# Fewer and larger pieces of the small products between the projections of the recurrent heads, with landing buffers of their own for the state-space branch's matrices

## The chip, the cores and the metric

The kernel runs on one NeuronCore of a Trainium2 chip. The metric is the device time of one execution in microseconds. All data is float32. Large products are made from two fp32r halves of each operand (a high part and the remainder), so that every product of two float32 matrices is three matmuls in fp32r; the small products are plain float32 matmuls, each of which the trace shows as two matmul instructions (a transpose shows as one).

## The reference, cut to what matters

Two transformer-like blocks follow each other on 512 tokens of width 1024. The change lies in the second one, in the stage between its input projection and its gates:

```python
z = rmsnorm(h, mix_norm_g[l])
p = z @ w_in[l]                                   # 1024 -> 1024 + 4 * 1024 + 2 * 1024 columns
y_a = s5_mixer(p[..., :o1], ...)                  # the branch: a state-space recurrence
y_b = hgrn2_mixer(p[..., o1:o2], p[..., o2:o3], p[..., o3:o4], p[..., o4:o5], ...)   # q, f, i, og of 8 heads
merged = (sigmoid(p[..., o5:o6]) * (y_a @ w_ssm_proj[l])
          + sigmoid(p[..., o6:]) * (y_b @ w_hgrn_proj[l]))
```

Each of the 8 heads has width 128: f gives a decay, its running sum within chunks gives the scaled q and k, and scores, a state per chunk and an output follow. The branch takes u, the first 1024 columns, in 64 groups of 16, turns it into v (`R` times u), runs a complex recurrence over 64 steps, and multiplies back (`MO`: two 128x128 matrices per group, one for u and one for the state).

## The kernel before, in words

Everything on the core is 528 columns wide here (16 meta tokens and 512 tokens). The stage runs so:

- **u** (L1171 to L1182): four weight loads of 256 columns, 8 products, each `prod2`. `prod2` (L1116) makes one 128x528 product as two halves of 264 (or 258) columns, each with 8 k steps; a k step is the three matmuls of `mm3` (L126 to L128) and then a call of `slot` (L1104).
- **heads** (the loop at the end of the stage, `for hd in range(9)`): for each of 8 heads two weight loads of two 1024x128 matrices each (`load_w2`, L119), then `head`: the products f, og, i, q, that is 4 x 16 = 64 k steps, with the scalar and vector work of the head between them (L1275 to L1321). What is left of a head, `back` (transposes of v and of the outgoing k, scores, states, outputs, the norm, a transpose back), is a generator that is stepped while the next head's products run.
- **gates** (hd = 8): 8 weight loads, 16 products, 256 k steps, beside the last head's `back`.

`slot` steps the generators in `self.fillers`. `back` is stepped at every k step, the branch at every third one (heads 1 to 4, `s5_state`) or at every one (heads 5 to 7, `s5_out`). Each step traces a few instructions up to its next `yield`. What is not finished at the end of a head is flushed there. The generator `s5_state` has 11 pieces of matmuls on R (L1205; each 24 matmul instructions and a copy, L1206) and then 64 steps of four vector operations (L1217 to L1220). `s5_out` has 16 copies of the states by ACT (L1230), then the MO products (L1247, L1248, copy L1249), a Gelu over the whole result (L1251) and 8 stores of y (`y_d`, L1253), through POOL's queue.

The queues don't follow the traced order strictly: the layer that builds the program orders each engine's instructions itself, by the traced order and by when it reckons operands and buffers to be there, and fixes that order in the program. Each engine then runs its list in order.

Buffers: raw weights land in `wraw` (two of 1 MB); `raw()` (L86) gives every third request a place in `xraw`, one more buffer of 1 MB that exists in this stage only. R and MO ask the same `raw()`: 6 loads of 768 KB for R and 10 of up to 896 KB for MO. Weights are split by ACT (`wh`, L131) and DVE (`wl`, L132) into three buffers each. `aux` is four PSUM banks for all small products, `pp` two double banks for the projections. All these loads are issued by SP (SyncE), in the order of its list; a load waits there until its buffer is free.

Of the kernel before, what the change touches and what calls it, by code (L numbers as in the profile page):

```python
# [19 lines left out]
P = 128  # L20
# [49 lines left out]
class Kern:  # L70
# [1057 lines left out]
    def block2(self):  # L1128
# [39 lines left out]
        self.xraw, self.nraw = hp, 2  # L1168
# [20 lines left out]
        def s5_state():  # L1189
            nonlocal Hs  # L1190
            v_ = slot(2).rearrange("p a b -> p (a b)").rearrange("p (c r g) -> p c r g", c=66, r=2)
            for c0 in range(0, 32, 3):
                n = min(3, 32 - c0)
                if c0 % 6 == 0:
                    rbase = 2 * c0
                    ng = min(12, 64 - rbase)
                    Rt = self.raw().rearrange("p (g x) -> p g x", x=P)
                    nc.sync.dma_start(Rt[:, :ng], self.R_d[:, rbase : rbase + ng])
                ps = self.aux()
                p4 = ps[:, : 2 * n * 66].rearrange("p (r g c) -> p r g c", r=2, g=n)  # L1200
                for i in range(2 * n):
                    g = 2 * c0 + i
                    for r in range(2):
                        par = i % 2
                        nc.tensor.matmul(p4[64 * par : 64 * par + 64, r, i // 2], lhsT=Rt[:, g - rbase, 64 * r : 64 * r + 64], rhs=U[:, g], start=True, stop=True)  # L1205
                nc.scalar.copy(v_[:, :, :, c0 : c0 + n].rearrange("p c r g -> p r g c"), p4)  # L1206
                yield
            self.tap("v", v_)
            Hs = slot(3).rearrange("p a b -> p (a b)").rearrange("p (c r g) -> p c r g", c=66, r=2)
            e = nc.vector  # L1210
            e.tensor_copy(Hs[:, 0], v_[:, 0])
            ar = self.a8[:, 0:1, :].to_broadcast([P, 2, 32])
            ai = self.a8[:, 1:3, :]
            for c in range(1, 65):
                t1 = self.tmp.tile([P, 2, 32], F32, tag="st1", bufs=2, name=self.nm("st1"))
                t2 = self.tmp.tile([P, 2, 32], F32, tag="st2", bufs=2, name=self.nm("st2"))
                e.tensor_tensor(t1, Hs[:, c - 1], ar, ALU.mult)  # L1217
                e.tensor_tensor(t2, Hs[:, c - 1, ::-1, :], ai, ALU.mult)
                e.tensor_tensor(t1, t1, v_[:, c], ALU.add)
                e.tensor_tensor(Hs[:, c], t1, t2, ALU.add)  # L1220
                yield

        def s5_out():
            SS = slot(2).rearrange("p a b -> p (a b)").rearrange("p (g c) -> p g c", c=66)
            nc.gpsimd.memset(SS[:, :, 0:1], 0.0)
            for par in range(2):
                for r in range(2):
                    for c0 in range(0, 65, 17):
                        c1 = min(65, c0 + 17)
# [6 lines left out]
            for g0 in range(0, 64, 7):  # L1236
                n = min(7, 64 - g0)
                MO = self.raw().rearrange("p (g s x) -> p g s x", s=2, x=P)
                nc.sync.dma_start(MO[:, :n].rearrange("p g s x -> p g (s x)"), self.MO_d[:, g0 : g0 + n])
# [9 lines left out]
                nc.scalar.copy(Y[:, g0 : g0 + n], ps[:, : n * 66].rearrange("p (g c) -> p g c", g=n))  # L1249
            yield  # L1250
# [73 lines left out]
        def back(hd, I, KO, K1, KX, Q1, QI, dec, og):  # L1324
# [4 lines left out]
            def tok(src, s, out):  # L1329
                pt_ = self.aux()  # L1330
                for c in range(NT):
                    nc.tensor.transpose(pt_[:, c * P : c * P + P], ch(src)[:, c], self.ident)
                    if c % 2:
                        yield
# [6 lines left out]
                out += [o, om]  # L1341

# [7 lines left out]
            for c in range(NT):  # L1350
                for i in range(4):
# [3 lines left out]
                    if i % 2:  # L1355
                        yield
# [7 lines left out]
            yield  # L1364
# [4 lines left out]
            for c in range(3):  # L1369
                yield  # L1370
# [5 lines left out]
            for _ in range(3):  # L1376
                yield
# [22 lines left out]
            for _ in range(16):  # L1400
                yield
# [29 lines left out]
        for hd in range(9):  # L1431
            self.fillers = [[prev, 1], [s5, 3 if hd < 5 else 1]]
# [17 lines left out]
        self.xraw = None  # L1450
# [165 lines left out]
    def run(self):  # L1616
        tc, nc = self.tc, self.nc
        with ExitStack() as es:
# [8 lines left out]
            self.nraw, self.xraw = 0, None  # L1627
# [48 lines left out]
```

## Time and profile before

| | us |
|---|---|
| median of 3 runs (1820.84 to 1827.03) | 1825.83 |
| the profiled execution, its own time | 1825.45 |
| its span, first to last instruction | 1823.6 |
| PE (TensorE) busy | 1738.0 (95%) |
| DVE busy | 1074.7 (59%) |
| ACT busy | 780.4 (43%) |
| POOL busy | 321.4 (18%) |

Mean granted TensorE clock: 0.986 of full speed.

How to read it: a view of the waits names an engine's instruction, what released it, the idle time in total, how often and the longest. A view of windows gives, for a stretch, its length, the busy time of each engine with the number of instructions, then the granted clock and the DMA share. In a timeline a row begins with start and duration, and an idle time before it stands in brackets with what ended it. The duration of a matmul is that of one that is pipelined with its neighbours, so the cost of a run of matmuls is read from start to start. The chain lists what the end of the program waited for, in order of time.

### The profile page before, as it was taken

The numbers are of one execution on the slowest core, as the hardware profiler recorded it, in microseconds if no ns is written. First come the engines' busy times: TensorE is split into PE (matmuls) and PEld (weight loads), VectorE is DVE, ScalarE is ACT, GpSimd is POOL, SyncE is SP. The second block draws the span as 40 slices with busy tenths as digits, with TensorE's granted clock in tenths as the row PEclk, the third lists the DMA queues.
The fourth block names the chain that finished last, engine by engine and source line by source line (L and its number), as shares of the span: only waits on it lengthen the run. The fifth ranks groups of instructions, "written<-read, shape, count | busy, mean of one in ns | idle before, by whom it ended". The sixth has DMA issues, their size and how long they took to land.

```text
span 1823.6 us, 28508 instructions
## 1 busy us (share of the span) xinstructions
PE 1738.0 (95%) x11509; PEld 1525.5 (84%) x11509; DVE 1074.7 (59%) x2343; ACT 780.4 (43%) x1298; POOL 321.4 (18%) x441
## 2 busy tenths in 40 slices
PE   1989998999999999999999999999999999999998
PEld 1777755877777778899899899899999999889986
DVE  6687878986443566454488634343444466536652
ACT  2674485344332444324546834343322443324332
POOL 5000000278836841031000000200000000000001
PEclk9899998999999999999899999999999999999999
DMA  7323625353244325367432135936443222332231
GB/s 280 98 88 111 215 71 186 116 105 124 85 117 150 108 92 182 117 195 123 129 99 82 65 116 162 227 118 232 156 137 104 82 93 70 113 107 93 70 104 47
DMA packets 178766, 226.64 MB, mean 124 GB/s; under 512 B 10699, under 2 KB 146746, under 8 KB 175178
## 3 DMA queue, kind: packets, MB, share of 16 engines
q1 hardware_dynamic: 164256, 181.95, 31.5%
q0 software_dynamic: 10640, 38.19, 7.8%
q10 hardware_dynamic: 3738, 4.69, 0.7%
q8 instruction: 90, 1.47, 0.4%
q14 instruction: 42, 0.34, 0.1%
HBM read 196.29 MB, written 32.70 MB: 126 GB/s over the span
## 4 chain that ended last, share of the span: by engine, by line
PE 69%; issue 12%; DVE 9%; ACT 4%; DMA 4%; POOL 1%; ACTq 0%; SPq 0%; POOLq 0%; DVEq 0%
PE pp L126 18%; PE pp L127 17%; PE pp L128 17%; DVE wl L132 2%; DMA wraw<-in_w_in_dram 2%; PE pd L128 1%; PE pd L126 1%; PE pd L127 1%; PE aux L1072 1%; PE aux L1354 1%; PE aux L442 1%; PE aux L126 1%; PE aux L128 1%; PE aux L127 1%; PE pv L455 1%
## 5 line engine op out<-in xcount | busy, mean ns | idle before, releaser
L126 PE MATMUL pp<-s,wh 128*128 128x258 f32 (+2 forms) x1856 | 543.2, 293 | 8.6 <-ACT sg L1427 4.5
L127 PE MATMUL pp<-s,wh 128*128 128x258 f32 (+2 forms) x1856 | 527.9, 284 | 0.0
L128 PE MATMUL pp<-s,wl 128*128 128x258 f32 (+2 forms) x1856 | 525.5, 283 | 0.0
L132 DVE TENSOR_TENSOR wl<-wraw,wh 128x1024 fp32r<-128x1024 f32 (+4 forms) x260 | 302.9, 1178 | 190.4 <-ACT wh L131 189.4
L131 ACT CAST wh<-wraw 128x1024 fp32r<-128x1024 f32 (+4 forms) x260 | 245.0, 964 | 338.0 <-PE pp L127 203.4
L126 PEld LDWEIGHTS pp<-s,wh 128*128 128x128 f32 x1856 | 352.2, 190 | 13.3 <-ACT sg L1427 4.7
L127 PEld LDWEIGHTS pp<-s,wh 128*128 128x128 f32 x1856 | 352.9, 190 | 0.2 <-DVE s L333 0.2
L128 PEld LDWEIGHTS pp<-s,wl 128*128 128x128 f32 x1856 | 352.4, 190 | 0.1
L126 PE MATMUL pp<-h2H,wh 128*128 128x512 f32 x336 | 133.5, 397 | 2.4 <-DVE cy L846 2.4
L127 PE MATMUL pp<-h2L,wh 128*128 128x512 f32 x336 | 133.2, 396 | 1.1 <-DVE h2L L343 1.1
L128 PE MATMUL pp<-h2H,wl 128*128 128x512 f32 x336 | 132.1, 393 | 0.0
L126 PEld LDWEIGHTS pp<-h2H,wh 128*128 128x128 f32 x336 | 63.1, 188 | 20.1 <-ACT aH L131 2.8
L127 PEld LDWEIGHTS pp<-h2L,wh 128*128 128x128 f32 x336 | 63.0, 188 | 16.1 <-DVE h2L L343 2.2
L128 PEld LDWEIGHTS pp<-h2H,wl 128*128 128x128 f32 x336 | 63.2, 188 | 14.2
L126 PE MATMUL pp<-aH,wh 128*128 128x512 f32 x176 | 70.1, 398 | 0.0
L127 PE MATMUL pp<-aL,wh 128*128 128x512 f32 x176 | 69.8, 396 | 0.0
L128 PE MATMUL pp<-aH,wl 128*128 128x512 f32 x176 | 69.8, 396 | 0.0
L1592 POOL TENSOR_TENSOR ht<-ht,gf 128x512 f32<-128x512 f32 x4 | 5.7, 1438 | 344.7 <-ACT fsq L1590 344.7
L126 PE MATMUL pp<-wh,hH 128*128 128x512 f32 (+1 forms) x160 | 62.3, 389 | 1.2 <-ACT hH L525 1.2
L1556 DVE TENSOR_TENSOR xz<-pp,rb_f 128x516 f32<-128x516 f32 x44 | 30.6, 696 | 54.2 <-PE pp L128 54.2
L127 PE MATMUL pp<-wl,hH 128*128 128x512 f32 (+1 forms) x160 | 61.9, 387 | 0.5 <-DVE wl L132 0.5
L128 PE MATMUL pp<-wh,hL 128*128 128x512 f32 (+1 forms) x160 | 61.4, 384 | 0.0
(592 smaller groups left out, 3462.0 us busy)
## 6 DMA issues: line engine op xcount, KB each, us to landing
wraw<-in_w_up_dram SPq DMA_DIRECT2D x40, 1024.0 KB, 5.2
wada<-in_w_ada_dram SPq DMA_DIRECT2D x24, 1024.0 KB, 4.9
wraw<-in_w_in_dram SPq DMA_DIRECT2D x17, 1024.0 KB, 12.3
wraw<-in_w_down_dram SPq DMA_DIRECT2D x16, 704.0 KB, 4.6
wraw<-in_w_in_dram SPq DMA_DIRECT2D x22, 512.0 KB, 5.4
wraw<-in_w_down_dram SPq DMA_DIRECT2D x8, 1024.0 KB
wraw<-MO_d SPq DMA_DIRECT2D x6, 896.0 KB
xraw<-in_w_in_dram SPq DMA_DIRECT2D x10, 512.0 KB, 7.7
```

The costliest lines, as they stand in the source:

```text
L126: mm(ps, lhsT=sh, rhs=mh, start=start, stop=False)
L127: mm(ps, lhsT=sh, rhs=ml, start=False, stop=False)
L128: mm(ps, lhsT=sl, rhs=mh, start=False, stop=stop)
L131: self.nc.scalar.copy(H, x)
L132: self.nc.vector.tensor_tensor(L, x, H.bitcast(F32), ALU.subtract)
L442: nc.tensor.transpose(ps[:, w : w + P], probs[i][:, j * P : (j + 1) * P], self.ident)
L455: self.nc.tensor.matmul(pv[64 * a : 64 * a + 64, j * P :], lhsT=vs[a](j), rhs=ptrs[a][j], start=(j == 0), stop=(j == NT - 1), skip_group_c ...
L1072: nc.tensor.matmul(pk[:16, i * P : i * P + P], lhsT=W[:, gi, 0, :], rhs=Ca[:, gi, :8, :].rearrange("p l h -> p (l h)"), start=True, stop=True)
L1354: nc.tensor.matmul(p3[:n, c, 32 * i : 32 * i + 32], lhsT=lhs, rhs=ch(Q1)[:, c, 32 * i : 32 * i + 32], start=True, stop=True)
L1556: nc.vector.tensor_tensor(xz, ps, rb, ALU.mult)
L1592: nc.gpsimd.tensor_tensor(h, h, gf[:, :512], ALU.mult)
```

## The change

`raw()` loses its third buffer, so that weights land in the two `wraw` buffers only. R and MO get a tag of their own, `xr`, two buffers of 512 KB: R now comes in 11 loads of up to 384 KB and MO in 16 loads of 512 KB, each asked for one piece ahead. A generator now says with `yield n` after how many k steps it wants to go on. The pieces of `back` are joined: all four transposes of a matrix, two chunks of scores, the three states, two chunks of outputs. The MO products go by 4 groups instead of 7, in one piece. The core of the diff:

```diff
     def raw(self):
-        self.nraw += 1
-        if self.xraw is not None and self.nraw % 3 == 2:
-            return self.xraw.tile([P, WCAP], F32, tag="xraw", bufs=1, name=self.nm("xraw"))
         return self.wpool.tile([P, WCAP], F32, tag="wraw", bufs=self.wbufs[0], name=self.nm("wraw"))
...
         self.nslot += 1
         for f in list(self.fillers):
-            if self.nslot % f[1] == 0 and next(f[0], self) is self:
-                self.fillers.remove(f)
+            if self.nslot >= f[1]:
+                w = next(f[0], 0)
+                f[1] = self.nslot + w
+                if w == 0:
+                    self.fillers.remove(f)
...
+            def r_load(c0):
+                n = min(3, 32 - c0)
+                Rt = hp.tile([P, 1024], F32, tag="xr", bufs=2, ...)
+                nc.sync.dma_start(Rt, self.R_d[:, 2 * c0 : 2 * c0 + 2 * n])
+                Rts.append(Rt)
+            r_load(0)
             for c0 in range(0, 32, 3):
                 n = min(3, 32 - c0)
-                if c0 % 6 == 0:
-                    ...
-                    Rt = self.raw().rearrange("p (g x) -> p g x", x=P)
-                    nc.sync.dma_start(Rt[:, :ng], self.R_d[:, rbase : rbase + ng])
+                Rt = Rts.pop(0)
+                if c0 + 3 < 32:
+                    r_load(c0 + 3)
...
                 nc.scalar.copy(v_[:, :, :, c0 : c0 + n].rearrange("p c r g -> p r g c"), p4)
-                yield
+                yield 2
...
                 e.tensor_tensor(Hs[:, c], t1, t2, ALU.add)
-                yield
+                yield 3
...  s5_out: after each of 16 copies (L1230)
-                        for _ in range(4):
-                            yield
+                        yield 2
...
-            for g0 in range(0, 64, 7):
-                n = min(7, 64 - g0)
-                MO = self.raw().rearrange("p (g s x) -> p g s x", s=2, x=P)
-                nc.sync.dma_start(MO[:, :n]..., self.MO_d[:, g0 : g0 + n])
-                for _ in range(8):
-                    yield
+            mo_load(0)
+            for g0 in range(0, 64, 4):
+                if g0 + 4 < 64:
+                    mo_load(g0 + 4)
+                yield 7
+                MO = MOs.pop(0)
                 ps = self.aux()
-                for i in range(n):
-                    if i % 2 == 0:
-                        yield
+                for i in range(4):
                     ...
-            yield
+            yield 6
             nc.scalar.activation(Y, Y, AF.Gelu_apprx_tanh)
...  back: transposes (L1332), scores (L1354), states (L1371), outputs (L1382)
-                    if c % 2:
-                        yield
...
+                yield 4
...
-                    if i % 2:
-                        yield
+                if c == 1:
+                    yield 4
...
-                yield
                 nc.tensor.matmul(s3[:, c + 1], lhsT=KT[:, c], rhs=VT[:, c], start=True, stop=True)
...
-            for _ in range(3):
-                yield
+            yield 5
...
                 nc.tensor.matmul(o3[:, c], lhsT=ch(QI)[:, c], rhs=Sx[:, c], start=False, stop=True)
-                yield
+                if c == 1:
+                    yield 4
...
-            for _ in range(16):
-                yield
+            yield 22
...
-            self.fillers = [[prev, 1], [s5, 3 if hd < 5 else 1]]
+            self.fillers = [[prev, self.nslot + 3], [s5, self.nslot + 1]]
```

Per head, `back` had a piece at nearly each of the first 24 k steps and its last one at the 40th; now it has 7 pieces at the k steps 3, 7, 11, 15, 19, 24 and 28 and the last one at 50. The branch's state part takes 22 + 192 = 214 k steps instead of 225, its output part 32 + 112 + 6 = 150 instead of some 185 (from the start of head 5).

## Rows read from the trace of the kernel before

**Rows 1.** PE's waits from 832 to 1252 us: in total, times, longest.
```profile
PE pp L126 <- ACT sg L1427: 4.5, 1, 4.5
PE aux L1404 <- DVE KT L1397: 3.9, 4, 2.8
PE pp L126 <- ACT wh L131: 3.5, 1, 3.5
```
**Rows 2.** Windows by stage: length, PE, PEld, DVE, ACT, POOL busy, clock, DMA.
```profile
880.00:905.00 25.00, 21.05 (x325) 17.53 (x320) 15.75 (x56) 15.19 (x25) 0.00 (x0) 0.90 0.53 158
905.00:940.00 35.00, 34.69 (x260) 32.37 (x261) 27.93 (x117) 19.00 (x28) 1.13 (x2) 0.93 0.48 136
...
1008.00:1045.00 37.00, 34.17 (x264) 32.00 (x263) 22.16 (x66) 34.11 (x43) 2.39 (x5) 0.95 0.20 68
...
1176.00:1180.00 4.00, 2.32 (x11) 2.32 (x12) 2.36 (x2) 2.12 (x4) 1.08 (x2) 0.54 1.06 380
1180.00:1186.00 6.00, 6.00 (x40) 6.00 (x40) 0.09 (x1) 1.30 (x2) 0.00 (x0) 0.74 1.03 387
1186.00:1200.00 14.00, 14.00 (x119) 14.00 (x119) 11.14 (x10) 10.98 (x12) 1.62 (x3) 1.00 0.30 110
```
**Rows 3.** The chain from 890 to 906 us: start, us, what.
```profile
896.26 7.67 DMA xraw<-in_w_in_dram
```
**Rows 4.** SP's queue from 780 to 920 us, in order.
```profile
882.64 0.32 SPq L1198 DMA_DIRECT2D xraw<-R_d  x1
...
895.82 1.73 SPq L119 DMA_DIRECT2D xraw<-in_w_in_dram  x2
```
**Rows 5.** PE's timeline just after that wait: two successive matmuls.
```profile
906.74 0.42 PE L127 MATMUL pp<-s,wh 128*128 128x264 f32 x1
906.96 0.42 PE L128 MATMUL pp<-s,wl 128*128 128x264 f32 x1
```
**Rows 6.** The chain at the gates; the stores of y (DMA issues).
```profile
1138.31 3.74 ACT s L1251
...
1146.48 28.58 DMA wraw<-in_w_in_dram
...
y_d<-s POOLq DMA_DIRECT2D x8, 264.0 KB, 17.2
```
**Rows 7.** Branch copies on ACT by line, and timeline rows of head 5.
```profile
L1230 ACT COPY s<-s 64x544 f32<-64x544 f32 (+1 forms) x16 | 17.3, 1121 | 2.7 <-DVE ss L1389 2.5
...
1032.81 0.60 ACT L1278 ACTIVATE og<-pp 128x516 f32<-128x516 f32 x1
...
1034.79 0.65 PE L1404 MATMUL aux<-ident,KT 128*128 128x128 f32 x4 [2.83 <-DVE KT L1397]
```
**Rows 8.** PE's timeline: a chunk of scores among products, and one without.
```profile
911.03 0.37 PE L126 MATMUL pp<-s,wh 128*128 128x264 f32 x1
...
912.78 0.37 PE L126 MATMUL pp<-s,wh 128*128 128x264 f32 x1
...
882.54 0.25 PE L1354 MATMUL aux<-E,LM 128*32 128x32 f32 x2
...
883.46 0.25 PE L1354 MATMUL aux<-E,LM 128*32 128x32 f32 x2
```
**Rows 9.** PE's timeline: an MO piece, a k step, the next piece.
```profile
1073.22 0.34 PE L1247 MATMUL aux<-U,xraw 128*128 128x66 f32 x2
...
1074.03 0.37 PE L126 MATMUL pp<-s,wh 128*128 128x264 f32 x1
...
1074.49 0.33 PE L1247 MATMUL aux<-U,xraw 128*128 128x66 f32 x2
```
**Rows 10.** PE's timeline: the first piece of R (24 matmul instructions).
```profile
879.61 0.97 PE L1205 MATMUL aux<-U,xraw 128*64 128x66 f32 x24
```
**Rows 11.** Landing times: weights and MO in the extra buffer, by DMA issues.
```profile
xraw<-in_w_in_dram SPq DMA_DIRECT2D x10, 512.0 KB, 7.7
...
xraw<-MO_d SPq DMA_DIRECT2D x3, 896.0 KB, 4.6
```

More of the change, by code (lines that the diff above doesn't have):

```diff
@@ L1191, in s5_state @@
             v_ = slot(2).rearrange("p a b -> p (a b)").rearrange("p (c r g) -> p c r g", c=66, r=2)
+            Rts = []
+            def r_load(c0):
+                n = min(3, 32 - c0)
+                Rt = hp.tile([P, 1024], F32, tag="xr", bufs=2, name=self.nm("xr"))[:, : 256 * n].rearrange("p (g x) -> p g x", x=P)
+                nc.sync.dma_start(Rt, self.R_d[:, 2 * c0 : 2 * c0 + 2 * n])
+                Rts.append(Rt)
+            r_load(0)
             for c0 in range(0, 32, 3):
                 n = min(3, 32 - c0)
-                if c0 % 6 == 0:
-                    rbase = 2 * c0
-                    ng = min(12, 64 - rbase)
-                    Rt = self.raw().rearrange("p (g x) -> p g x", x=P)
-                    nc.sync.dma_start(Rt[:, :ng], self.R_d[:, rbase : rbase + ng])
+                Rt = Rts.pop(0)
+                if c0 + 3 < 32:
+                    r_load(c0 + 3)
                 ps = self.aux()
@@ L1204, in s5_state @@
                         par = i % 2
-                        nc.tensor.matmul(p4[64 * par : 64 * par + 64, r, i // 2], lhsT=Rt[:, g - rbase, 64 * r : 64 * r + 64], rhs=U[:, g], start=True, stop=True)
+                        nc.tensor.matmul(p4[64 * par : 64 * par + 64, r, i // 2], lhsT=Rt[:, i, 64 * r : 64 * r + 64], rhs=U[:, g], start=True, stop=True)
                 nc.scalar.copy(v_[:, :, :, c0 : c0 + n].rearrange("p c r g -> p r g c"), p4)
-                yield
+                yield 2
             self.tap("v", v_)
@@ L1230, in s5_out, with mo_load @@
                         nc.scalar.copy(SS[64 * r : 64 * r + 64, par::2, 1 + c0 : 1 + c1], Hs[64 * par : 64 * par + 64, c0:c1, r].rearrange("p c g -> p g c"))
-                        for _ in range(4):
-                            yield
+                        yield 2
             self.tap("SS", SS)
             Y = slot(3).rearrange("p a b -> p (a b)").rearrange("p (g c) -> p g c", c=66)
-            for g0 in range(0, 64, 7):
-                n = min(7, 64 - g0)
-                MO = self.raw().rearrange("p (g s x) -> p g s x", s=2, x=P)
-                nc.sync.dma_start(MO[:, :n].rearrange("p g s x -> p g (s x)"), self.MO_d[:, g0 : g0 + n])
-                for _ in range(8):
-                    yield
+            MOs = []
+            def mo_load(g0):
+                MO = hp.tile([P, 1024], F32, tag="xr", bufs=2, name=self.nm("xr")).rearrange("p (g s x) -> p g s x", s=2, x=P)
+                nc.sync.dma_start(MO.rearrange("p g s x -> p g (s x)"), self.MO_d[:, g0 : g0 + 4])
+                MOs.append(MO)
+            mo_load(0)
[4 more added lines that the diff above has]
+                MO = MOs.pop(0)
                 ps = self.aux()
-                for i in range(n):
-                    if i % 2 == 0:
-                        yield
+                for i in range(4):
                     o = ps[:, i * 66 : i * 66 + 66]
@@ L1248, in s5_out @@
                     nc.tensor.matmul(o, lhsT=MO[:, i, 1], rhs=SS[:, g0 + i], start=False, stop=True)
-                nc.scalar.copy(Y[:, g0 : g0 + n], ps[:, : n * 66].rearrange("p (g c) -> p g c", g=n))
-            yield
+                nc.scalar.copy(Y[:, g0 : g0 + 4], ps[:, : 4 * 66].rearrange("p (g c) -> p g c", g=4))
+            yield 6
             nc.scalar.activation(Y, Y, AF.Gelu_apprx_tanh)
@@ L1383, in back @@
                 nc.tensor.matmul(o3[:, c], lhsT=ch(QI)[:, c], rhs=Sx[:, c], start=False, stop=True)
-                yield
+                if c == 1:
+                    yield 4
             pm = self.aux()
@@ L1399, in back @@
             vec.tensor_scalar(onm, pm[:4, :P], rs[:4, 4:5], None, ALU.mult)
-            for _ in range(16):
-                yield
+            yield 22
             pt_ = self.aux()
@@ L1449, in block2 @@
         self.fillers = []
-        self.xraw = None
         es3.close()
@@ L1626, in run @@
             self.act_norm = (2, 3)
-            self.nraw, self.xraw = 0, None
             self.es_z = ExitStack()
```

1 line of the change is left out of this document (removed).

## The prediction

> **What bounds the kernel now.** I read the windows first, to see which stages leave PE idle or at the lower clock level, then PE's own waits there, then for each wait the chain or the queue that ended it. PE is the bound nearly everywhere; the stage of the change (832 to 1252 us) holds three places where it isn't.
>
> *Place A, the start of head 2.* PE waits 3.5 us for the weights' high part [rows 1], and the chain shows behind it a weight load that was issued at 896.26 and took 7.67 us [rows 3]. SP's list says why so late: the load stands behind loads of R, in the buffer that R held [rows 4]; R in turn waited for PE's first R piece, at 879.61 [rows 10]. After the wait the granted clock is lower: 0.90 over 25 us and 0.93 over 35 us [rows 2] are 2.5 / 0.5 + 2.45 / 0.5 = 9.9 us at 1.2 GHz, some 8 us of them with work, in which products start 0.22 us apart [rows 5] instead of 14.00 / 119 = 0.118 [rows 2]. That loses 8 x (1 - 0.118 / 0.22) = 3.7 us. A is worth 7.2 us.
>
> *Place C, the gates.* The chain holds one weight load that took 28.58 us, while the eight stores of y, whose median landing is 17.2 us, were under way [rows 6]. PE waits 4.5 us [rows 1] (behind ACT, which was stuck on the split of those weights), and 4 x 0.46 / 0.5 + 6 x 0.26 / 0.5 = 6.8 us are at the lower level [rows 2], some 5.3 with work: 5.3 x 0.46 = 2.5. C is worth 7.0 us.
>
> *Place B, head 5.* The 16 branch copies take 17.3 us of ACT [rows 7], which is busy 34.1 of 37 us [rows 2]. The sigmoid of og comes at 1032.81, DVE's work behind it is late, and PE waits 2.83 us for it [rows 7]; the clock, 0.95 over 37 us, is 3.7 us at the lower level and loses 1.7. B is worth 4.5 us.
>
> The other waits on L1404 are 3.9 - 2.8 = 1.1 us [rows 1]. All told 19.8 us, of a profiled execution of 1825.45 us (span 1823.6; the median of the runs is 1825.83, so the sum carries over with 0.4 us).
>
> **The change part by part.**
>
> *Landing places.* R and MO no longer stand in the weights' buffers. Head 2's two loads then need only head 1's splits and a free `wh`, both there before head 1 ends, so the wait on them goes. Two weight buffers are enough: a head needs 2 MB in over 30 us, and one 512 KB piece lands in 7.7 us at the median [rows 11]. Next in line at A is R itself. U lands too late for the first pieces of head 1, so that all 11 pieces wait, and they were run in a bunch from 879.61 on, about 0.9 us each [rows 10]. Before, three buffers held 6 of the 11 pieces ahead; now two buffers hold 2, and 9 loads must come during the bunch, two in flight. The trace has no load of 384 KB; the nearest are MO's 896 KB at 4.6 us and 512 KB of weights at 7.7 us, both in company [rows 11]. At 4.6 us a pair of pieces takes about 5.5 us and nine pieces 25 us, of which 8 are their own products: 17 us to fill. To fill them there are 8 to 10 us of head 0's delayed pieces and now the f product of head 2 (48 matmuls x 0.12 = 5.8 us), whose weights are there: 14 to 16 us. At 7.7 us it is 31 us to fill, with 15 uncovered, which would turn A's gain of 7.2 into a loss of about 8. I take the 4.6 us end, since these loads are the smaller ones: A gives -6, between -7.2 and +8.
>
> MO: its 16 loads are asked for two pieces ahead, that is 14 k steps of 0.36 us and one piece of 1.8 us later, 6.8 us in all, against 4.6 us for a larger load [rows 11]. Hidden; in the worst case, 7.7 us, 0.9 us x 14 = 13 us would show, but the heads' own pieces lengthen the 14 steps, so I count nothing.
>
> A rule of the Trainium skill speaks against halving the loads ("DMA: Bandwidth & Descriptors", "Anatomy of one DMA"): each DMA costs about 2 us whatever its size. By an estimate from that page 384 KB would land in 2.9 us, so that the loads would be hidden and A would be -7; no run here shows a load of that size.
>
> *The branch's timetable.* The output part ends about 35 k steps earlier (at 150 instead of 185 of heads 5 to 7), so the Gelu and the y stores move from the last steps of head 7 to its first third. The stores then run against nothing urgent: the first two gate loads no longer queue behind MO, and can land before. I take -6.5 of C's 7.0, ends -7.0 and 0. What is late next is the Gelu itself, 3.74 us of ACT [rows 6] in the middle of a head; I allow 0 to 4 us for it inside the range, and take 0.
>
> The 16 copies come at every second k step instead of every fourth. All 16 now rank ahead of og's sigmoid (k step 32), where before 8 did. ACT's total is the same and its second half of the head becomes free. I take 0 for B, ends -4.5 (the copies are over before ACT is needed) and +9 (below).
>
> *Larger pieces.* The number of small matmuls is the same, so only what a switch costs can be saved. Scores: a chunk in two pieces with two k steps costs 912.78 - 911.03 = 1.75 us, less six products of 0.12, that is 1.03 us; the same chunk in one go costs 883.46 - 882.54 = 0.92 [rows 8]. 0.11 x 4 chunks x 8 heads = 3.5 us. MO: a piece of 8 matmuls takes 1074.03 - 1073.22 = 0.81 us, and the k step behind it 0.46 instead of 0.36 [rows 9]: 0.91 us for 8, 0.114 each, about what each product costs anyway; half as many pieces save at most 16 x 0.1 = 1.6 us. The transposes and outputs are 128 columns wide like MO, and I count nothing for them. I take -3 in all, ends 0 and -7 (all the rest saving 0.1 us per joined piece).
>
> A rule of the Trainium skill bears on this ("TensorEngine Tiling (Array Packing)", "Key Properties"): changing the tiling mode drains TensorE. The scores go through the widths 32, 64, 96 and 128 in every chunk, joined or not, so by that rule nothing would be saved here and the sum would be 3 us smaller.
>
> The norm: the last piece of `back` now waits 22 k steps instead of 16, but the trace already has it later than traced, where DVE was reckoned to be ready, and the waits of 1.1 us remain: 0, ends -1 and +1.
>
> *Sum:* -6 (A) - 6.5 (C) + 0 (B) - 3 (pieces) = -15.5 us. 1825.45 - 15.5 = 1810.
>
> **The rivals.**
>
> 1. *R streams too slowly.* C and the pieces give 9.5, but the bunch at A waits for its loads. For it: two landing places for 9 loads, at a time when PE has little else. Against it: head 2's f product is free to run. With A at 0 it is 1816, with A at +4, 1820.
>
> 2. *The change hardly does what it says.* The engines' lists are ordered by what is reckoned to be ready, not by the traced k steps: all R pieces stand in a bunch in spite of their steps. If the y stores still meet the gates' loads (C 0) and only A or the pieces come, it is 1820 to 1826: no change that can be told.
>
> 3. *Slower: ACT in head 5.* The six copies that stood behind og's sigmoid are put ahead of it: 6 x 1.12 = 6.7 us [rows 7]. The q product needs the PSUM that og's product holds, and PE already waits behind og [rows 7], so there is no slack: some 6 us more, and 2 to 3 at the lower clock, +9; the Gelu in head 7 blocks in the same way, up to +4 and a further 2. It makes the kernel slower only where A isn't gained either: -6.5 (C) + 15 = 1832 to 1836. It decides from the point where og's sigmoid starts more than 3 us later, counted from the head's start, than before.
>
> 4. *More:* the pieces give 7 and B goes too: 1800.
>
> **How the numbers follow.** Forecast (A and C gone, 1804 to 1814): 0.50. Rival 1 (1814 to 1820): 0.20. Rival 2: 0.14. Rival 3: 0.10. Rival 4: 0.06. 0.3% is 5.5 us, about what a measurement of this kernel can tell from no change. Faster by more than that (below 1820.3): 0.50 + 0.06 + 0.18 of rival 1 = 0.74; within: 0.16; slower: 0.10. The range takes forecast, rival 1, most of rival 2 and the nearer part of rival 4: 1800 to 1825. It leaves out rival 3 and the ends.
>
> **What would show it.** In the changed profile: no wait of PE on `wh` at head 2 and no lower clock there (A right); waits of PE before L1205 on a DMA of `xr` (rival 1). y's stores at about 1110 to 1135, and no wait of PE at the gates (C right). Four transposes or 16 score matmuls in a row, with a cost per score chunk near 0.92 us (pieces). og's sigmoid in head 5 relative to the copies, and ACT's share there (B, rival 3). The forecast is wrong if PE is still idle around 880 to 905 us, or if a new wait of over 5 us stands in heads 5 or 7.

## The result, and where the time went

The change makes the kernel slower: 1837.33 us (median of 8 runs, 1830.66 to 1846.43) against 1826.43 (8 runs, 1820.84 to 1831.25), a ratio of 1.0063 with a 95% interval of 1.0045 to 1.008, +10.9 us. The forecast was 1810. The profiled execution took 1839.34 us (span 1837.2), that of before 1825.45.

I cut both traces at the same four events: the start of the F sigmoid of heads 0 and 5, and of the first and the last sigmoid of the gates. The windows of before, of a second profile of the same kernel (`e0_same`, below), and of the changed kernel; the rows are the time ahead of head 0, heads 0 to 4, heads 5 to 7 and the gates (columns as in [rows 2]: stretch, its length, busy time of PE, PEld, DVE, ACT and POOL, clock, DMA share, GB/s):

```profile
0.00:838.20 838.20, 773.48 (x3913) 605.08 (x3914) 555.72 (x1279) 384.25 (x754) 282.86 (x384) 0.98 0.42 135
838.20:1020.60 182.40, 177.23 (x1572) 165.52 (x1571) 126.38 (x490) 97.31 (x144) 9.46 (x16) 0.97 0.45 105
1020.60:1152.50 131.90, 128.76 (x1055) 122.70 (x1053) 60.10 (x153) 72.88 (x101) 9.34 (x14) 0.99 0.42 124
1152.50:1250.10 97.60, 93.12 (x756) 92.37 (x756) 32.19 (x44) 33.25 (x42) 10.15 (x18) 0.97 0.60 168
```

```profile
0.00:845.10 845.10, 779.24 (x3914) 608.88 (x3914) 557.02 (x1279) 384.27 (x755) 282.30 (x384) 0.98 0.42 134
845.10:1024.70 179.60, 175.17 (x1572) 164.06 (x1571) 126.11 (x490) 97.21 (x143) 9.42 (x16) 0.99 0.46 106
```

```profile
0.00:845.00 845.00, 780.16 (x3913) 610.20 (x3914) 555.95 (x1279) 384.12 (x754) 282.50 (x384) 0.97 0.42 134
845.00:1032.40 187.40, 178.55 (x1562) 168.36 (x1562) 122.97 (x481) 91.52 (x136) 9.25 (x15) 0.95 0.43 97
1032.40:1167.70 135.30, 129.29 (x1060) 124.36 (x1059) 63.56 (x162) 79.89 (x114) 9.64 (x15) 0.97 0.58 144
1167.70:1263.80 96.10, 93.12 (x761) 92.12 (x760) 32.09 (x47) 33.09 (x43) 10.12 (x18) 0.98 0.43 147
```

Ahead of head 0 the kernel before itself took 838.2 us in one profile and 845.1 in the next: the 6.8 us that the changed kernel seems to lose there are scatter. The loss is in the heads: 187.4 us against 182.4 and 179.6 in heads 0 to 4, 135.3 against 131.9 and 132.0 in heads 5 to 7. The gates gain nothing against the second profile (95.9).

The waits of PE in the stage of the changed kernel, which answer to [rows 1]:

```profile
PE aux L1258 <- ACT s L1236: 6.0, 1, 6.0
PE aux L1211 <- DMA xr<-R_d: 5.3, 1, 5.3
PE pp L123 <- ACT sg L1434: 3.0, 1, 3.0
PE pp L123 <- ACT I L1328: 1.3, 1, 1.3
PE aux L1411 <- DVE KT L1405: 1.2, 2, 0.7
PE aux L1346 <- ACT VT L1344: 1.0, 1, 1.0
```

The waits for `wh` and for the norm's 2.8 us are gone. In their place stand a wait for R's load, in the place of A, and one for the branch's copies, in head 5: these are the two signs that I had named for a wrong forecast (PE idle around 880 to 905 us, a new wait of over 5 us in heads 5 or 7).

R's matmuls and the last of the recurrence's four operations, by line (duration, first and last start); before, then changed:

```profile
L1205 PE MATMUL aux<-U,wraw x160: 222/222/273, 883.8 to 898.1; 128*64 128x66 f32 x160
L1205 PE MATMUL aux<-U,xraw x96: 222/222/273, 879.6 to 895.6; 128*64 128x66 f32 x96
L1220 DVE TENSOR_TENSOR s<-st,st x64: 201/216/228, 900.1 to 1015.0; 128x64 f32<-128x64 f32 x64
```

```profile
L1211 PE MATMUL aux<-U,xr x256: 220/222/374, 885.4 to 919.2; 128*64 128x66 f32 x128
L1226 DVE TENSOR_TENSOR s<-st,st x64: 199/208/231, 921.8 to 1032.9; 128x64 f32<-128x64 f32 x64
```

R's pieces took 18.5 us (879.6 to 898.1) and now take 33.8. The recurrence behind them runs over 110 to 115 us either way (its four operations keep DVE busy for at most 55 of them; its steps are traced three k steps apart, with the heads' work between), so it ends later: in the kernel before 5.6 us ahead of head 5's F sigmoid (1020.6), in the changed one 0.5 us after it (1032.4). What that does to ACT in head 5, against [rows 7]:

```profile
1032.44 0.61 ACT L1285 ACTIVATE F<-pp 128x528 f32<-128x528 f32 x1 [5.43 <-PE pp L125]
1033.88 14.66 ACT L1236 COPY s<-s 64x544 f32<-64x544 f32 x14
...
1051.52 0.60 ACT L1288 ACTIVATE og<-pp 128x516 f32<-128x516 f32 x1
```

14 copies in a row; og's sigmoid comes 19.1 us after F's, where it was 12.2 (1020.6 to 1032.8). PE stands at its first MO piece for 6.0 us, since that needs the copies.

The granted clock, against [rows 2]. The first four rows are stretches at the lower level, in heads 2 and 3, at the wait in head 5 and at that on R, the fifth a further one among R's pieces; the last shows the 32 score matmuls in a row (L1363 alone) in which the first of these stretches began:

```profile
934.22:941.05 6.83, 6.83 (x34) 6.33 (x34) 4.68 (x27) 0.40 (x1) 0.00 (x0) 0.50 0.11 41
964.94:968.35 3.41, 3.41 (x16) 3.41 (x17) 1.69 (x12) 0.00 (x0) 0.00 (x0) 0.50 1.07 296
1050.30:1057.10 6.80, 5.55 (x25) 5.55 (x26) 5.40 (x20) 6.72 (x9) 0.00 (x0) 0.50 0.25 77
893.30:900.10 6.80, 4.41 (x40) 4.01 (x42) 1.47 (x4) 2.53 (x4) 0.00 (x0) 0.50 0.59 186
906.90:910.30 3.40, 3.40 (x32) 3.05 (x31) 0.54 (x3) 0.85 (x1) 0.00 (x0) 0.50 0.22 35
...
931.66:936.03 4.37, 4.37 (x32) 3.79 (x32) 0.79 0.31 121
```

In the kernel before the clock stayed at 1.0 through heads 2 to 4 but for the rest of place A. Heads 0 to 4 have 20.5 us at the lower level in the changed kernel, 10.2 and 3.4 in the two profiles of before. So the stalls have moved: to R's stream, to head 5 and to new drops of the clock, of which the ones at 906.9, 934.2 and 964.9 each come during or just after 32 scores in a row.

### The profile page after: what moved, and what is told of

The parts are those of the page before. It is cut to its first block, busy times and chain, and to the rows that moved or that the text cites. A ratio compares the mean times of both kernels' runs of the same rounds, so it can differ in the third digit from the quotient of the medians.

```text
span 1837.2 us, 28548 instructions
## 1 busy us (share of the span) xinstructions
PE 1746.5 (95%) x11509; PEld 1534.9 (84%) x11509; DVE 1075.0 (59%) x2343; ACT 781.3 (43%) x1304; POOL 321.1 (17%) x441
## 3 DMA queue, kind: packets, MB, share of 16 engines
q1 hardware_dynamic: 165840, 181.95, 31.5%
## 4 chain that ended last, share of the span: by engine, by line
PE 75%; issue 12%; DVE 6%; ACT 3%; DMA 3%; POOL 1%; ACTq 0%; SPq 0%; POOLq 0%; DVEq 0%
PE pp L123 19%; PE pp L124 18%; PE pp L125 18%; PE aux L1363 2%; PE pd L125 1%; PE pd L123 1%; PE pd L124 1%; PE aux L1069 1%; PE aux L439 1%; PE pv L452 1%; PE aux L123 1%; PE aux L125 1%; PE aux L124 1%; DVE wl L129 1%; ACT s L1236 1%
## 5 line engine op out<-in xcount | busy, mean ns | idle before, releaser
L129 DVE TENSOR_TENSOR wl<-wraw,wh 128x1024 fp32r<-128x1024 f32 (+4 forms) x276 | 322.3, 1182 | 183.1 <-ACT wh L128 181.9
L128 ACT CAST wh<-wraw 128x1024 fp32r<-128x1024 f32 (+4 forms) x276 | 261.0, 969 | 350.1 <-PE pp L124 237.1
L123 PE MATMUL pp<-h2H,wh 128*128 128x512 f32 x336 | 134.1, 399 | 2.4 <-DVE cy L843 2.4
```

What stands on the lines that cost most here:

```text
L123: mm(ps, lhsT=sh, rhs=mh, start=start, stop=False)
L128: self.nc.scalar.copy(H, x)
L129: self.nc.vector.tensor_tensor(L, x, H.bitcast(F32), ALU.subtract)
```

## The experiments

All ratios are to runs of the kernel before on the same chip; the three last columns are cut at the events above, in us.

| kernel | ratio (95%) | heads 0-4 | heads 5-7 | gates |
|---|---|---|---|---|
| before; again: e0_same | 1.0003 (0.9987 to 1.0019) | 182.4; 179.6 | 131.9; 132.0 | 97.6; 95.9 |
| changed | 1.0063 (1.0045 to 1.008) | 187.4 | 135.3 | 96.1 |
| again: s1_after | 1.0083 (1.0057 to 1.0109) | 187.7 | 135.2 | 96.1 |
| e1_land | 1.0055 (1.0033 to 1.0077) | 178.1 | 144.0 | 93.2 |
| e2_pieces | 1.0033 (1.0018 to 1.0049) | 175.2 | 139.2 | 95.7 |
| e3_small | 1.007 (1.0044 to 1.0095) | 188.2 | 136.9 | 93.7 |
| e5_rpool | 1.0054 (1.0035 to 1.0073) | 188.1 | 135.4 | 96.0 |
| e6_late | 1.0063 (1.0038 to 1.0088) | 188.2 | 137.6 | 96.1 |
| e4_rhalf | 0.9995 (0.9981 to 1.0009) | 178.9 | 129.8 | 94.5 |
| again: s2_rhalf | 1.0 (0.9981 to 1.0019) | 179.0 | 129.7 | 94.5 |
| e7_both | 0.9986 (0.9971 to 1.0002) | 178.8 | 129.9 | 94.5 |
| e8_small | 0.998 (0.9966 to 0.9995) | 183.6 | 127.3 | 95.2 |
| e10_oldout | 0.9977 (0.9961 to 0.9994) | 180.0 | 131.3 | 95.4 |
| e11_late | 0.999 (0.9974 to 1.0006) | 178.5 | 137.0 | 96.1 |
| again: s3_late | 1.0015 (0.9997 to 1.0033) | 174.7 | 134.1 | 96.1 |
| s4_gates | 1.0005 (0.999 to 1.0021) | 180.5 | 132.0 | 92.9 |
| e9_gates | 0.9957 (0.9938 to 0.9975) | 178.3 | 129.2 | 91.3 |
| again: f1_best | 0.9959 (0.9943 to 0.9974) | 178.6 | 130.8 | 91.3 |
| f2_shift | 0.9975 (0.996 to 0.9989) | 181.0 | 134.8 | 91.3 |

The group e8 to e11 shares a sample of the kernel before with a median of 1827.75 us, where the other groups had 1823 to 1825, so ratios of that group may be 0.001 to 0.0025 too low against other groups (the group s1 to s4 ran on the same chip, with 1823.07 for the kernel before).

**Landing places or pieces?** Three kernels, each with a part of the change. `e1_land` is the kernel before with the landing places alone:

```diff
-                if c0 % 6 == 0:
...
-                    Rt = self.raw().rearrange("p (g x) -> p g x", x=P)
+                Rt = Rts.pop(0)
+                if c0 + 3 < 32:
+                    r_load(c0 + 3)
```

> The kernel before with the landing places alone: R's 11 loads (384 KB) and MO's 16 (512 KB) go to two places of their own, the weights to theirs; all pieces and their spacing stay as before. Queue theory (R's third load stands in SP's list behind some ten weight loads that wait for their own places): PE waits 3 to 6 us for xr in head 1 or 2, the recurrence of the branch ends 8 to 15 us later than before, and the time is 5 to 10 us above before (1831 to 1837). Theory of the pieces (the landing places are harmless, the loss is the larger pieces and the lower clock after them): no wait on xr over 2 us, and 1820 to 1827.

`e2_pieces` is the kernel before with the joined pieces of `back`, their waits and their start alone:

```diff
-                    if i % 2:
-                        yield
+                if c == 1:
+                    yield 4
...
-            for _ in range(16):
-                yield
+            yield 22
```

> The kernel before with the larger pieces of the heads' own small products alone, with their new waits (4, 5 and 22 k steps) and their start at the third k step; landing places and the branch stay as before. Theory of the pieces: the granted clock falls to the lower level after the bunches of scores in heads 2 and 3, as it does in the changed kernel, for 6.8 and 3.4 us, and the time is 3 to 6 us above before (1829 to 1832). Queue theory: the pieces do next to nothing, within 3 us of before (1823 to 1829). My forecast had them at -3.

`e3_small` is the changed kernel with this part undone:

```diff
-            yield 22
+            for _ in range(16):
+                yield 1
```

> The changed kernel with the heads' own small products cut as before (one piece per k step, 16 k steps before the last one, start at the first); landing places and the branch's timetable stay as changed. Theory of the pieces: granted clock 1.0 in heads 2 and 3, and 4 to 6 us under the changed kernel (1831 to 1833). Queue theory: the wait on xr (5.3 us) and the wait on the branch's copies in head 5 (6.0 us) stay, and the time is within 3 us of the changed kernel (1834 to 1840).

Both halves alone lose, and undoing the pieces gains nothing. The landing places alone gain in heads 0 to 4 (178.1), with no wait on `xr`, but R's pieces take 25.9 us, the recurrence ends 8.8 us after head 5's F sigmoid, and heads 5 to 7 lose 12. The pieces alone gain in heads 0 to 4 (175.2), and since the heads get ahead of the recurrence, it ends with head 5's F sigmoid (1017.4 and 1017.3), and heads 5 to 7 lose 7. That the recurrence's end is the cause there too is argued, not shown. The drops of the clock in heads 2 and 3 that the theory of the pieces asked for did not come, so its time was met by another route. In both kernels most of the loss is a long stretch at the lower clock around the first MO pieces; `e2_pieces`, `e1_land`, and two stretches of before over the same work:

```profile
1049.70:1070.20 20.50, 20.50 (x98) 19.34 (x97) 4.20 (x12) 5.50 (x6) 0.00 (x0) 0.50 0.28 90
```

```profile
1055.40:1072.50 17.10, 17.10 (x80) 15.77 (x80) 3.39 (x7) 2.26 (x4) 0.00 (x0) 0.50 0.52 155
```

```profile
1047.00:1060.00 13.00, 12.68 (x104) 11.25 (x102) 3.11 (x8) 1.85 (x6) 0.00 (x0) 1.00 0.22 72
1060.00:1076.00 16.00, 16.00 (x137) 15.64 (x138) 11.04 (x37) 10.57 (x17) 0.00 (x0) 1.00 0.36 117
```

In `e3_small` 32 scores stand in a row in heads 2 and 3 although they were traced in fours, and the clock falls there for 6.8 us each time: the layer that orders the lists makes that bunch. With R in time there is one such bunch, in head 2, whether the pieces are large (`e4_rhalf`) or small (`e8_small`), and none in the kernel before. `e1_land` and `e3_small` differ only in the branch's timetable (R at every third or at every second k step, and what follows it): at every third, head 2's f product is through early (F's sigmoid at 891.0, R from 888.5), at every second PE waits 5.2 us for `xr`. (Its wait of 5.0 us on the norm stands in head 5, behind 12 of the branch's copies in a row on ACT, in the place of the changed kernel's 6.0.) So the two places seem too few for pieces that follow at every second step. One profile of each carries this last point.

**Queue or places?** SP's list holds R's third load behind ten weight loads (issue start, stretch, count):

```profile
842.53 47.35 SPq L116 DMA_DIRECT2D wraw<-in_w_in_dram  x10
889.99 26.17 SPq L1196 DMA_DIRECT2D xr<-R_d  x9
```

`e5_rpool` takes R's loads out of it:

```diff
-                nc.sync.dma_start(Rt, self.R_d[:, 2 * c0 : 2 * c0 + 2 * n])
+                nc.gpsimd.dma_start(Rt, self.R_d[:, 2 * c0 : 2 * c0 + 2 * n])
```

> The changed kernel with one word changed: R's loads are issued by GpSimd's queue instead of SP's. Two landing places and all sizes stay. Queue theory: R's third load is issued as soon as the first place is free, the wait of 5.3 us on xr goes or falls under 1.5 us, the last R piece is over 5 to 20 us sooner, the recurrence ends before head 5 begins, the wait of 6.0 us on the copies there falls under 2 us, and the time is 6 to 11 us under the changed kernel (1826 to 1831). Rival 1 of the forecast (two places are too few for the stream): waits on xr stay at 3 to 6 us in all, and the time is within 3 us of the changed kernel.

The queue theory falls. R's pieces take as long:

```profile
L1211 PE MATMUL aux<-U,xr x256: 222/222/371, 878.6 to 913.5; 128*64 128x66 f32 x128
```

34.9 us, with 3.7 us of waits on `xr` left, the 6.0 us in head 5 unchanged, and a ratio that can't be told from the changed kernel's. PE is idle for only 5.0 of the 34.9 us, and in the changed kernel for 6.6 of the 33.8: the rest of the length is PE's list, which has f's products and the heads' own pieces between R's pieces. `e4_rhalf` leaves the queue and gives R room instead, in the place that the recurrence's result takes later:

```diff
+            Rb = slot(3).rearrange("p a b -> p (a b)")
+            for c0 in range(0, 15, 5):
+                nc.sync.dma_start(Rb[:, 256 * c0 : 256 * c0 + 1280].rearrange("p (g x) -> p g x", x=P), self.R_d[:, 2 * c0 : 2 * c0 + 10])
...
-            r_load(0)
+            r_load(15)
+            r_load(18)
```

> The changed kernel with the first 15 of the 32 columns of R loaded ahead into the place that the recurrence's result takes later, and the next two pieces into the two landing places; only four loads are left to stream. Everything else as changed. Theory of the late R (two places make R's pieces take 34 us instead of 18, so that the recurrence ends with head 5's start instead of 5.4 us ahead of it, and the heads' own pieces in heads 2 and 3 fall into dense bunches behind which the clock drops): R's pieces take under 22 us, no wait over 1.5 us on xr, the recurrence ends 3 us or more before head 5's F, at most 3.4 us of the lower clock in heads 2 and 3, and the time is 7 to 11 us under the changed kernel's ratio of 1.0063: 1.000 to 1.0025. Theory of the pieces (the bunches come of the larger pieces themselves): the clock in heads 2 and 3 falls all the same, and the ratio is 1.004 to 1.008.

> The changed kernel with 15 columns of R ahead again, on the same chip as the changed kernel. If the late R is the whole loss, the ratio is 0.006 to 0.009 under that of the changed kernel, heads 0 to 4 take 178 to 180 us and heads 5 to 7 129 to 131. If the first comparison owed something to its chip, the distance is 0.002 to 0.005.

> The changed kernel again, beside the two below on one chip. If its first profile was typical: ratio 1.005 to 1.008, heads 0 to 4 in 186 to 189 us, heads 5 to 7 in 134 to 137, gates in 95 to 97. If that profile was an outlier, heads 0 to 4 come at under 184.

It gives the whole loss back: 0.9995 and 1.0, beside 1.0083 for the changed kernel on the same chip as the second. Its windows, R and the recurrence:

```profile
842.40:1021.30 178.90, 176.31 (x1587) 166.71 (x1586) 126.73 (x492) 99.74 (x146) 10.72 (x17) 0.98 0.46 107
1021.30:1151.10 129.80, 126.86 (x1034) 121.93 (x1033) 59.07 (x150) 69.66 (x106) 9.41 (x14) 0.97 0.55 135
1151.10:1245.60 94.50, 91.52 (x760) 90.53 (x759) 32.02 (x46) 33.01 (x43) 10.11 (x18) 1.00 0.43 149
```

```profile
L1215 PE MATMUL aux<-U,xr x136: 222/222/273, 891.7 to 903.7; 128*64 128x66 f32 x136
L1215 PE MATMUL aux<-U,s x120: 222/222/273, 883.7 to 889.8; 128*64 128x66 f32 x120
L1230 DVE TENSOR_TENSOR s<-st,st x64: 196/215/225, 905.4 to 1009.9; 128x64 f32<-128x64 f32 x64
```

20.0 us for R, and the recurrence ends 11.4 us ahead of head 5's F sigmoid. The repeats of these two kernels agree with their first profiles to 0.3 us in every stage. Of the 15.7 us between them, heads 0 to 4 hold 8.6, heads 5 to 7 5.5, the gates 1.6. Of the 8.6, 6.3 are idle time of PE (187.4 - 178.55 us in the changed kernel, 178.9 - 176.31 here). One expectation missed: head 2 keeps 6.8 us at the lower level, behind its bunch of 32 scores.

**Is it the recurrence's end?** `e11_late` keeps R in time and makes the recurrence late again:

```diff
+            yield 30
             for c in range(1, 65):
```

> The changed kernel with 15 columns of R ahead (ratio 0.9995), and 30 k steps of waiting ahead of the recurrence, so that it ends late again although R's pieces are in time. Theory of the late recurrence: all copies stand behind head 5's F on ScalarE's list again, og's sigmoid in head 5 comes 17 to 19 us after F's instead of 12.8, heads 0 to 4 keep their 179 us and heads 5 to 7 take 133 to 136 instead of 129.8: ratio 1.001 to 1.003. If the copies' place doesn't matter (the loss in heads 5 to 7 came of R or of the clock): heads 5 to 7 stay under 131.5, ratio under 1.0005.

> R in time and the recurrence 30 k steps later, again, on the same chip. If the late recurrence in head 5 is the larger part (first profile: heads 5 to 7 in 137.0 us against 129.7, gates in 96.1 against 94.5), the ratio is 0.003 to 0.005 above that of R in time. If R's stream in heads 0 to 4 is the larger part (178.5 us here against 187.4 in the changed kernel), the ratio is at most 0.002 above that of R in time, and 0.004 to 0.007 under the changed kernel.

Head 5 on ACT:

```profile
1022.82 0.61 ACT L1290 ACTIVATE F<-pp 128x528 f32<-128x528 f32 x1 [5.43 <-PE pp L125]
1023.32 14.68 ACT L1241 COPY s<-s 64x544 f32<-64x544 f32 x14
...
1040.98 0.60 ACT L1293 ACTIVATE og<-pp 128x516 f32<-128x516 f32 x1
```

That is the changed kernel's head 5 again: 14 copies, og's sigmoid 18.2 us after F's, PE waiting 5.4 us for the copies, heads 5 to 7 in 137.0 and 134.1 us against 129.7, gates in 96.1 against 94.5. So the mechanism is shown. Its net price is less than that of R: the time is 0.0015 above R in time on the same chip, within what can be told (the first timing, 0.999, missed the expected 1.001 to 1.003), and one profile gave 4 us back in heads 0 to 4.

`e6_late` tried the other cure, later copies with R as changed, `e7_both` joins it with R ahead:

```diff
+            yield 32
             for par in range(2):
...
-                yield 7
+                yield 5
```

> The changed kernel with 32 k steps of waiting ahead of the branch's first copy in head 5, and 5 instead of 7 k steps between MO's pieces. Rival 3's mechanism (ACT's 14 copies in a row at head 5's start hold up og's sigmoid by 7 us and PE by 6.0 us): og's sigmoid in head 5 comes 10 to 13 us after F's instead of 19.1, the wait on the copies goes, and heads 5 to 7 take 130 to 132 us instead of 135.3, so 3 to 5 us less: ratio 1.0035 to 1.005. If those waits only move (MO's pieces are denser then, and y's stores no earlier): heads 5 to 7 take 134 to 138 us, ratio 1.005 to 1.008.

> The two edits together: 15 columns of R loaded ahead, and the copies 32 k steps into head 5 with MO's pieces every fifth step. By the theory of the late R with rival 3's mechanism the gains add up, 10 to 16 us under the changed kernel: ratio 0.997 to 1.001, heads 0 to 4 in 176 to 180 us and heads 5 to 7 in 130 to 132. If one of the two theories is wrong, it is where the other one alone is; if both are, 1.004 to 1.008.

With R late it gives nothing: og's sigmoid in head 5 comes at 13.5 us, but the wait on the copies is still 4.6 us and heads 5 to 7 take 137.6. With R ahead it adds 0.001, not more than can be told.

**The other terms, with R in time.** `e8_small` cuts the heads' pieces small again, `e10_oldout` puts the branch's output on the old timetable (edits as in `e3_small`, and `yield 2` back to four single steps).

> The changed kernel with 15 columns of R ahead (ratio 0.9995), and the heads' own small products cut as before: one piece per k step, 16 k steps before the last one. It prices the larger pieces by themselves, with R in time. My forecast had them at -3 us: then this kernel is 2 to 4 us above the one with the larger pieces, ratio 1.0005 to 1.002. If a joined piece saves nothing (16 scores in a row cost 1.74 to 1.84 us in the changed kernel, 0.11 each, about what they cost in fours between k steps), the ratio is 0.9985 to 1.0005. If the larger pieces cost something by the lower clock behind them: 0.997 to 0.9985.

> The changed kernel with 15 columns of R ahead (ratio 0.9995), and the branch's output part by the old timetable: copies at every fourth k step, MO's pieces of two products pairs at single steps, so that the Gelu and the stores of y come some 25 us later and meet the gates' loads again. My forecast had place C at 6.5 us: ratio 1.002 to 1.004, gates in 98 to 101 us against 94.5. If the earlier stores are worth only what the gates showed so far (94.5 to 96 us against 95.9 and 97.6 in the kernel before), the ratio is 0.9995 to 1.001.

In the traces the larger pieces gain 4.6 us in heads 0 to 4 (183.6 to 179.0) and lose 2.4 in heads 5 to 7, the new timetable gains 1.0, 1.6 and 0.9: sums of 2.9 (with 0.7 in the gates) and 3.5. The times show neither (medians of 1823.0 us each, beside 1822.1 for `s2_rhalf` on the same chip), so both are at most a few us. The expected 98 to 101 us in the gates of `e10_oldout` missed: they take 95.4, with 2.5 us of wait on sg, although its Gelu comes 26.1 us after head 7's F sigmoid, nearly as late as before.

**The gates.** The wait of 3.0 us on sg stands in the changed kernel although y's stores are over by then (its Gelu starts at 1129.8, 38 us ahead of the first gate; before 14 us). ACT there, changed kernel, then before:

```profile
1189.19 1.99 ACT L128 CAST wh<-wraw 128x1024 fp32r<-128x1024 f32 x2 [9.77 <-PE pp L124]
1191.09 0.62 ACT L128 CAST yH<-og 128x516 fp32r<-128x516 f32 x1
1191.61 1.09 ACT L1434 ACTIVATE sg<-pp 128x516 f32<-128x516 f32 x2
```

```profile
1175.14 1.99 ACT L131 CAST wh<-wraw 128x1024 fp32r<-128x1024 f32 x2 [9.08 <-DMA wraw<-in_w_in_dram]
1177.03 1.08 ACT L1427 ACTIVATE sg<-pp 128x516 f32<-128x516 f32 x2
```

The same cast stands ahead of the same two sigmoids. It waited for the load, and now waits for PE to leave its place in `wh`; PE meanwhile needs the PSUM that the sigmoids free. The Trainium skill says that ScalarE's queue is strictly first in, first out ("TensorE: Matmul & The Clock Gate", "Architectural detail: the array is 16× 32×32, not 1× 128×128"); these rows agree. `e9_gates` (on `e7_both`) and `s4_gates` (on the kernel before) move that cast to VectorE:

```diff
+        if self.dve_split:
+            self.nc.vector.tensor_copy(H, x)
+        else:
+            self.nc.scalar.copy(H, x)
```

> The kernel with both edits (R ahead, copies later; ratio 0.9986), and in the gates the high part of the weights is cut on VectorE instead of ScalarE. The wait of 3.0 us in the gates stands in every changed kernel, whether y's stores are long over or not. If ScalarE's list makes it (a cast of weights that waits for PE to free its place stands ahead of the sigmoids that free PE's PSUM), the wait goes, the gates take 91 to 92.5 us instead of 94.5, and the ratio is 0.996 to 0.998. If the weights' places themselves are the bound, the wait moves to another line, the gates take 94 to 96, and the ratio is 0.998 to 1.000.

> The kernel before with one thing changed: in the gates the high part of the weights is cut on VectorE instead of ScalarE. If ScalarE's list holds the sigmoids behind a cast that waits, as in the changed kernels, the wait on sg (4.5 and 3.6 us in the two profiles of before) falls under 1.5 us, the gates take 92 to 94 us instead of 95.9 to 97.6, and the ratio is 0.997 to 0.9985. If y's stores are what counts, as my forecast had it, the weights come as late as before, the wait only changes its name, and the ratio is 0.999 to 1.001.

> The kernel with 15 columns of R ahead, the copies later and the gates' cut on VectorE, again. If its three gains are real: ratio 0.995 to 0.998, stage from F's first sigmoid to the last gate in 397 to 401 us, gates in 91 to 92. If the first time owed its distance to the sample of the kernel before: 0.998 to 1.0.

> The same with 12 k steps of waiting ahead of the recurrence. If VectorE's recurrence holds up heads 1 to 4 (one profile of the kernel with the recurrence 30 k steps later had heads 0 to 4 in 174.7 us against 179), heads 0 to 4 take 175 to 177 us and heads 5 to 7 129 to 131: ratio 0.001 to 0.002 under the kernel beside it. If that profile was scatter: 178 to 179, and a ratio within 0.001.

`f1_best`, the gates:

```profile
1147.10:1238.40 91.30, 91.30 (x760) 90.52 (x760) 37.66 (x57) 23.85 (x32) 10.10 (x18) 1.00 0.50 169
```

PE is busy without a gap. This kernel beats both others: 0.9957 and 0.9959, some 7.5 us under before and 19 or more under the changed one. Alone on the kernel before the edit shortens the gates by 3 to 4.7 us in the trace (92.9), and the times don't show it (0.999 to 1.0021): that stays open. `f2_shift`, the recurrence 12 k steps later, is worse in heads 0 to 7, and `e11_late`, the same kernel as `s3_late`, had 178.5 with 10.2 us at the lower level where `s3_late` has 3.4, so the 174.7 was scatter.

`e0_same` is the control, and shows how far one profile may be trusted:

> The kernel before, unchanged, for a second profile of it. If what comes ahead of the stage is scatter, its first F sigmoid lies anywhere from 838 to 845 us, as it does in the kernels run so far (838.2, 841.2, 842.1, 843.2, 845.0), and the ratio is 1.000 within 0.002. If the time ahead of the stage belongs to the changed kernels, it lies at 837 to 839 us, as in the first profile (838.2).

## Why the prediction was wrong, step by step

Against the mean of the two profiles of before, the changed kernel (two profiles) is 6.5 us longer in heads 0 to 4, 3.3 longer in heads 5 to 7 and 0.7 shorter in the gates: 9.2 in sum, for 10.9 and some 15 timed. With R ahead it is -2.0, -2.2 and -2.3.

- **A, -6: wrong, at +6.5 with the pieces' part.** Right: the wait on `wh` at head 2 went, and R itself came next. The step that failed is "To fill them there are 8 to 10 us of head 0's delayed pieces and now the f product". PE runs its list in order, and the list put R's third piece ahead of most of f's matmuls (7 of 48 had run): PE stood 5.3 us and went on with f behind it.

```profile
887.02 0.97 PE L1211 MATMUL aux<-U,xr 128*64 128x66 f32 x24
889.28 0.39 PE L123 MATMUL pp<-s,wh 128*128 128x264 f32 x1 [1.28 <-ACT I L1328]
...
895.69 1.61 PE L1211 MATMUL aux<-U,xr 128*64 128x66 f32 x24 [5.30 <-DMA xr<-R_d]
```

  The load behind that wait took longer than the 4.6 us I took; the chain has it, beside two weight loads:

```profile
889.99 5.56 DMA xr<-R_d
```

  Others were quicker: the one whose landing the issue view has took 3.9 us, and the ten of 384 KB in `e5_rpool`, on GpSimd's queue, 4.0 at the median. The Trainium skill's figure ("DMA: Bandwidth & Descriptors", "Anatomy of one DMA"; given there for DMAs that GpSimd issues) made an estimate of 2.9, some 1.1 too short. From the end of the second piece to the end of the last one (888.0 to 919.5) R took 31.5 us, where I had 25 for the nine pieces. Then the clock: the place itself has 10.2 us at the lower level as in the first profile of before, and the drops behind the scores in heads 2 and 3 are another 10.2, some 4.7 us by my rate of 0.46. That is rival 1 near its end of +8, to which I gave no chance of its own: I cut rival 1 off at +4. One reading under A was off without harm: the wait of 3.5 us ended at 901.8, with the first of two loads issued from 895.8 on; the one of 7.67 us landed at 903.9, after it.
- **What A left out.** I priced a late R by PE's wait alone and followed none of its users. R feeds the recurrence, which runs over 110 to 115 us and had 5.6 us to spare at head 5. This chain is in no wait of PE in the kernel before, so [rows 1] can't show it; the question "who waits for R's results, and with how much slack" would have.
- **B, 0: wrong, +3.3; rival 3.** Its sign came true: og's sigmoid in head 5 starts 6.9 us later than before, over my mark of 3, and the time of 1837 lies next to its 1832 to 1836. Its reason did not: I blamed copies at every second k step. With the same spacing and R in time og's sigmoid comes 12.8 us after F's; with R in time and the recurrence late, 18.2. Nor was the wait that of the q product: PE stood at MO's first piece.
- **C, -6.5: mis-sized, -0.7 here and -2.3 with R ahead.** The Gelu moved from 28.6 us after head 7's F sigmoid to 5.3 before it, as forecast, and the last store landed at 1162.5, ahead of the first gate's sigmoid. But I put the whole stall down to the load [rows 6]; the cast behind it blocks ACT's list all the same, and 3.0 of the 4.5 us stay, as 2.5 do in `e10_oldout` with late stores. And 4.5 was a bad draw: the second profile of before has 3.6.
- **Pieces, -3: not refuted.** 16 scores in a row cost 1.84 us, 0.92 a chunk as I had read from [rows 8]:

```profile
1161.82 1.84 PE aux L1363 x16
1165.18 1.84 PE aux L1363 x16
```

  With R in time they are worth 2.9 us in one pair of profiles. In the kernel before alone they lose (`e2_pieces`), probably since faster heads meet the recurrence's end.
- **The norm and the Gelu, 0:** right; 1.2 us of waits stay on the norm, none on the Gelu.
- **The base.** 19.8 us of stalls came from one profile. The second one lacks 2.8 us in heads 0 to 4 and 1.7 in the gates, without any edit.

With R in time the profiles give -6.5 us, the times -0.9 and 0.0 by the ratios (-1.5 and -1.0 by the medians), with some 3 us either way. So even without the late R at most half of the forecast 15.5 was there.

## What to carry to other kernels

Before giving a transfer fewer landing places, follow its data to the last user and note the slack there: here a stall of 5 us on PE came with 15 us of delay for a chain on another engine that had 5.6 to spare. A gap isn't filled by work that could run, only by work that the engine's own list has at that point. And take the worth of a stall from two profiles: here the first overstated two stages by 1.7 and 2.8 us.

## What the runs showed of the hardware

The clock fell with PE busy, and not only at waits. In the profiled kernels 32 score matmuls stand in a row 27 times; 23 times the granted clock fell to 0.50 during them or within 1.4 us behind them, for 3.4 or 6.8 us, with no wait of PE over 1.0 us beside them. Three times it did not fall, and once it was low already. The three profiles with scores in runs of at most 12 (before, `e0_same`, `s4_gates`) have drops in this stage only beside waits of 2.4 us or more.

How long the lower level lasted went with what PE did next. After waits of 2.1 us (`e1_land`) and 2.3 us (`e2_pieces`) it lasted 17.1 and 20.5 us at a PE that was busy all the time, with scores, MO pieces and single k steps. Behind a wait of 3.3 us in `e1_land` that 48 products followed it lasted 3.4 us, and beside the waits of 5.3 and 6.0 us in the changed kernel 6.8. The same mix ran for 29 us at full clock in the kernel before, where PE had come to it without such a wait just before. Two executions of one kernel differ by 6.9 us over the first 840, with 27.3 us of them at the lower level in the one and 41.0 in the other.
